# Encoder block on one core: the down projection's right-hand block sums are made in the up projection's rounds and kept in DRAM, and VectorE does all two-operand work of the down projection

## The chip, the core and the metric

The kernel runs on one core of a Trainium2 chip. A core has TensorE (PE; its weight loads, PEld, run beside its matmuls), VectorE (DVE), ScalarE (ACT), GpSimd (POOL) and SyncE (SP), which issues all DMAs of this kernel in one queue. The metric is the device time of one execution in microseconds. The kernel before takes 1479.98 us, the median of three runs (1477.62, 1479.98, 1480.10).

## The reference

One encoder layer on 1024 tokens of width 1024, in float32: a mixer (convolution group and grouped attention), cross-attention into 256 memory tokens, and a gated MLP, each between two RMS norms. The change lies in the MLP:

```
u = h @ w_up                           # 1024 x 1024 by 1024 x 5632
u = depthwise_conv3(u) + b             # along the tokens
y = (gelu(u[:, :2816]) * u[:, 2816:]) @ w_down     # 2816 x 1024
x = x + rmsnorm(y, norm_ffn_post)
```

## The kernel before

Every float32 product is done as three matmuls of rounded parts: an operand x is split into hi (a cast on ScalarE) and lo = x - hi (a subtraction of two operands), and hi*hi, hi*lo and lo*hi are summed in PSUM.

Both MLP products use Winograd's form of Strassen's method on one level: seven products of half-size blocks instead of eight, at the price of sums of blocks.

**Up projection** (lines 829 to 845). Round fi of 22 makes 128 gate and 128 value channels for all tokens. `up_first(fi)` loads wg and starts two products (p1, p2); `up_operands(fi)` loads wv, builds four weight sums s12 and s34 on GpSimd (lines 775 to 778) and splits them (`a_split`, lines 741 to 743: the cast on ScalarE, lo on VectorE or GpSimd); a22, the split of wv's second half, lies in one tile for an even and the next odd round. `up_finish(fi - 1)` runs the five other products p6, p5, p3, p7, p4 of the round before, adds them up on VectorE from PSUM (line 803), does the convolution of three taps (lines 792 to 795), the gelu and the gating, and stores the result to act_d in DRAM. A product is 12 matmuls of 128x512.

**Down projection** (lines 850 to 1020). Products m1, m2, m6, m7, m5, m4, m3 follow one another. Each runs over 11 steps i; a step has one operand tile `op` (hi and lo of a left block, 128x512, and of a right block), used by 4 x 3 matmuls. `operands(name, i)` makes it. The left blocks come from `acts[i]`, read back from act_d, and are changed in place between products. The right blocks are b11, b12, b22, b21 of w_down and four sums of them: t1 = b12 - b11, b22 - b12, t2 = b22 - t1 and t2 - b21. b11 of all steps stays in SBUF (`t1s`, three tiles of the pool `act`) and becomes t1 in m6; the other blocks are staged per step (`stage_w`: two blocks) or per two steps (`stage_pair`: one block), and the sums are made there, on GpSimd and VectorE. From the fourth step on, the lo part of the right block is made on GpSimd (`engs`). The `done` functions add each product's PSUM into the Y tiles on VectorE; `y_half` squares a half for the norm and multiplies it by the gain, `y_out` scales, adds the residual and stores.

**Buffers.** `raw` has 3 tiles of 128x1024 (wg, wv, and staged blocks), `tmp` 4 (q, s12, s34, staged blocks, residuals), `w` 7 of 128x2048 (operands; up to four of them are Y tiles, so three are left for `op` from m6 on), `act` 15 of the same size. PSUM has four tiles of one bank (`psB`) and two of two banks. A framework orders each engine's instructions when the program is built, by the order in which the kernel names them and by its own estimate of when each can start; a tile is loaded again when its last reader has released it. On the chip each engine, SP's queue too, runs its instructions in that order and waits on semaphores.

Of the kernel before, what the change touches and what calls it, by code (L numbers as in the profile page):

```python
# [17 lines left out]
NF = 22  # L18
# [15 lines left out]
def encoder_block(ctx: ExitStack, tc: tile.TileContext, x, xT, mem, w_a, w_q, w_kv, w_mkv, w_mqT,  # L34
# [30 lines left out]
    def f(t):  # L65
        return t.bitcast(F32)
# [673 lines left out]

    def a_split(dst, src, eng):
        nc.scalar.copy(out=dst[:, 0, :], in_=src)  # L742
        eng.tensor_tensor(out=dst[:, 1, :], in0=src, in1=f(dst[:, 0, :]), op=ALU.subtract)  # L743
# [95 lines left out]
    for fi in range(NF + 1):  # L839
        if fi < NF:  # L840
            if fi >= UP_PRE:
                up_first(fi)
            up_operands(fi)
        if fi:
            up_finish(fi - 1)

# [5 lines left out]
    t1s, acts = [], []  # L852
    for i in range(NH):
        if i % 4 == 0:
            n = min(4, NH - i)
            t1s.append(A([4, 512], "t1s", F32))
            nc.sync.dma_start(out=t1s[-1][:, :n, :], in_=w_down[i:i + n, :, 0, :].rearrange("i p n -> p i n"))
        acts.append(A([4, 512], "acts", F32))
        nc.sync.dma_start(out=acts[i][:, 0:2, :], in_=act_d[i].rearrange("p (h t) -> p h t", h=2))
# [6 lines left out]
    def t1_of(i):  # L866
        return t1s[i // 4][:, i % 4, :]

    nst = [0]

    pairs = {}

    def stage_pair(i, b):

        if i % 2 == 0:
            n = min(2, NH - i)
            st = raw("st2").rearrange("p (i n) -> p i n", i=2)
            nc.sync.dma_start(out=st[:, :n, :], in_=w_down[i:i + n, :, b, :].rearrange("i p n -> p i n"))
            pairs[b] = st
        return pairs[b][:, i % 2, :]  # L880

    def stage_w(i, b, n):
        nst[0] += 1
        st = (tmp if nst[0] % 2 == 0 else raw)("st").rearrange("p (b n) -> p b n", b=2)
        nc.sync.dma_start(out=st[:, :n, :], in_=w_down[i, :, b:b + n, :])
        return st
# [6 lines left out]
    def operands(name, i):  # L893
        a11, a21, a12, a22 = [acts[i][:, b, :] for b in range(4)]
        t1 = t1_of(i)
        engs = (V_, V_ if i < 3 else P_)
        if name == "m1":
            s_, t_ = a11, t1
        elif name == "m2":
            s_, t_ = a12, stage_pair(i, 3)  # L900
        elif name == "m6":
            st = stage_w(i, 1, 2)
            comb(P_, t1, st[:, 0, :], t1)
            comb(V_, st[:, 1, :], st[:, 1, :], t1)
            s_, t_ = a11, st[:, 1, :]
        elif name == "m7":
            st = stage_w(i, 1, 2)
            comb(P_, st[:, 1, :], st[:, 1, :], st[:, 0, :])
            comb(V_, a11, a22, a11)
            s_, t_ = a11, st[:, 1, :]  # L910
        elif name == "m5":
            comb(P_, a21, a21, a22, ALU.add)
            s_, t_ = a21, t1
        elif name == "m4":
            st = stage_w(i, 2, 2)
            comb(P_, st[:, 0, :], st[:, 0, :], t1)
            comb(V_, st[:, 0, :], st[:, 0, :], st[:, 1, :])
            s_, t_ = a22, st[:, 0, :]
        else:
            s_, t_ = a12, stage_pair(i, 2)  # L920
        op = (A if name == "m3" and i >= NH - 3 else W)([4, 512], "op")
        for n, src in ((0, s_), (2, t_)):
            nc.scalar.copy(out=op[:, n, :], in_=src)  # L923
            comb(engs[n // 2], op[:, n + 1, :], src, f(op[:, n, :]))
        if name == "m2":
            comb(V_, a11, a22, a11)
            comb(P_, a11, a11, a21, ALU.add)
            comb(V_, a12, a12, a11)
# [35 lines left out]
    def y_half(t, n, y, dst=None):  # L964

        nc.scalar.activation(out=gF[:, 1, H0], in_=y, func=AF.Square, accum_out=ssF[n][:, t:t + 1])
        comb(V_ if n else P_, y if dst is None else dst, y, gF[:, 0, n * 512:n * 512 + 512], ALU.mult)
# [119 lines left out]
```

## Time and profile before

| | us |
|---|---|
| the profiled execution's own time | 1478.46 |
| its span, first to last instruction | 1476.7 |
| TensorE, matmuls | 1392.0 busy (94%) |
| VectorE | 1099.4 busy (74%) |
| ScalarE | 700.5 busy (47%) |
| GpSimd | 707.2 busy (48%) |
| mean granted TensorE clock | 0.983 of full speed |

Busy times are shares of the whole span, in which stages with different limits follow one another; the MLP's two products run from about 770 us to the end. Matmuls overlap one another in the records (0.39 us each, while they start closer together), so TensorE's pace is read from start to start. A wait row names who ended the wait. A group of instructions is named by its line and by the tiles that it writes and reads; line 891 is a helper (`comb`) that makes most two-operand work of the down projection, and line 743 is the second half of `a_split`.

### The profile page before, as it was taken

The numbers are of one execution on the slowest core, as the hardware profiler recorded it, in microseconds if no ns is written. First come the engines' busy times: TensorE is split into PE (matmuls) and PEld (weight loads), VectorE is DVE, ScalarE is ACT, GpSimd is POOL, SyncE is SP. The second block draws the span as 40 slices with busy tenths as digits, with TensorE's granted clock in tenths as the row PEclk, the third lists the DMA queues.
The fourth block names the chain that finished last, engine by engine and source line by source line (L and its number), as shares of the span: only waits on it lengthen the run. The fifth ranks groups of instructions, "written<-read, shape, count | busy, mean of one in ns | idle before, by whom it ended". The sixth has DMA issues, their size and how long they took to land.

```text
span 1476.7 us, 18881 instructions
## 1 busy us (share of the span) xinstructions
PE 1392.0 (94%) x7020; PEld 1165.0 (79%) x7020; DVE 1099.4 (74%) x1323; ACT 700.5 (47%) x1192; POOL 707.2 (48%) x627
## 2 busy tenths in 40 slices
PE   7999999889999999999997999999999997978895
PEld 5889988678988888888875888888888875756784
DVE  7499898899999534335468777777777789996676
ACT  6325653688888424334435444444444443323442
POOL 6628787711111414002137555444445449697456
PEclk9999999999999999999998999999999999999998
DMA  6316770000000524013223222222222292334145
GB/s 208 128 48 207 260 237 15 20 1 1 1 2 29 178 94 141 31 43 129 93 79 114 87 86 86 86 87 86 86 87 79 95 375 100 106 130 143 42 130 192
DMA packets 49515, 152.77 MB, mean 103 GB/s; under 512 B 9104, under 2 KB 9360, under 8 KB 49424
## 3 DMA queue, kind: packets, MB, share of 16 engines
q1 hardware_dynamic: 49424, 151.58, 30.8%
q8 instruction: 55, 0.90, 0.3%
q14 instruction: 36, 0.29, 0.1%
HBM read 119.05 MB, written 32.51 MB: 103 GB/s over the span
## 4 chain that ended last, share of the span: by engine, by line
PE 65%; DVE 15%; POOL 6%; issue 5%; DMA 5%; ACT 3%; SPq 0%; POOLq 0%; DVEq 0%; ACTq 0%
PE p L97 9%; PE p L98 9%; PE p L100 9%; DVE op L891 4%; PE y L98 4%; PE y L100 4%; PE y L97 4%; PE pPT L81 3%; PE sc L100 2%; PE sc L97 2%; PE sc L98 2%; DVE acts L891 2%; PE po L555 2%; PE sp L524 2%; PE sp L525 2%
## 5 line engine op out<-in xcount | busy, mean ns | idle before, releaser
L91 PE MATMUL yd<-op 128*128 128x512 f32 x308 | 126.8, 413 | 31.9 <-DVE op L891 16.0
L295 DVE SCALAR_TENSOR_TENSOR cacc<-conv,col,cacc 128x1009 f32<-128x1009 f32 (+14 forms) x120 | 145.8, 1273 | 4.7 <-ACT cacc L242 4.5
L92 PE MATMUL yd<-op 128*128 128x512 f32 x308 | 123.4, 404 | 1.8 <-DVE op L891 1.7
L923 ACT CAST op<-acts 128x512 fp32r<-128x512 f32 x77 | 47.6, 621 | 129.9 <-PE yd L92 47.6
L891 DVE TENSOR_TENSOR op<-acts,op 128x512 fp32r<-128x512 f32 x77 | 88.7, 1158 | 26.0 <-ACT op L923 25.8
L742 ACT CAST a<-s 128x512 fp32r<-128x512 f32 x88 | 50.6, 620 | 113.4 <-PE p L100 55.4
L91 PEld LDWEIGHTS yd<-op 128*128 128x128 f32 x308 | 60.2, 196 | 55.1 <-POOL op L891 23.5
L90 PE MATMUL yd<-op 128*128 128x512 f32 x308 | 98.4, 394 | 0.0
L743 POOL TENSOR_TENSOR a<-wg,a 128x512 fp32r<-128x512 f32 x44 | 62.5, 1441 | 72.9 <-ACT a L742 72.9
L793 DVE SCALAR_TENSOR_TENSOR c<-u,col,c 128x1023 f32<-128x1023 f32 x44 | 56.7, 1288 | 49.4 <-ACT c L792 49.3
L743 DVE TENSOR_TENSOR a<-s,a 128x512 fp32r<-128x512 f32 x88 | 72.3, 835 | 27.8 <-ACT a L742 27.5
L545 DVE TENSOR_TENSOR PL<-pPT,PH 128x512 fp32r<-128x512 f32 x128 | 82.7, 680 | 5.0 <-ACT PH L544 4.6
L85 POOL TENSOR_SCALAR rt<-ss 128x1 f32<-128x1 f32 (+1 forms) x43 | 13.0, 302 | 150.4 <-ACT x L609 75.8
L527 DVE TENSOR_REDUCE nm<-sp 128x1 f32<-128x1024 f32 x64 | 78.0, 1219 | 2.9 <-PE sp L525 1.8
L530 ACT ACTIVATE P<-sp,nm 128x1024 f32<-128x1024 f32 x64 | 72.2, 1128 | 8.9 <-PE pPT L81 5.1
L792 ACT ACTIVATE c<-u,col 128x1024 f32<-128x1024 f32 x44 | 53.2, 1210 | 48.7 <-DVE u L803 46.8
L544 ACT CAST PH<-pPT 128x512 fp32r<-128x512 f32 x128 | 69.3, 593 | 13.5 <-PE pPT L81 12.7
L92 PEld LDWEIGHTS yd<-op 128*128 128x128 f32 x308 | 60.1, 195 | 16.2 <-DVE op L891 4.2
L81 PE MATMUL pPT<-ident,P 128*128 128x128 f32 x512 | 68.6, 274 | 3.7 <-DVE PL L545 2.3
L90 PEld LDWEIGHTS yd<-op 128*128 128x128 f32 x308 | 58.8, 191 | 12.6
L81 PEld LDWEIGHTS pPT<-ident,P 128*128 128x128 f32 x512 | 58.6, 140 | 12.3 <-DVE PL L545 3.9
L743 POOL TENSOR_TENSOR a<-wv,a 128x512 fp32r<-128x512 f32 x22 | 31.9, 1468 | 74.6 <-ACT a L742 60.5
(352 smaller groups left out, 4553.7 us busy)
## 6 DMA issues: line engine op xcount, KB each, us to landing
st<-in_w_down_dram SPq DMA_DIRECT2D x43, 512.0 KB, 3.8
wg<-in_w_up_dram SPq DMA_DIRECT2D x22, 512.0 KB, 4.1
wv<-in_w_up_dram SPq DMA_DIRECT2D x22, 512.0 KB, 3.9
act_d<-u SPq DMA_DIRECT2D x22, 512.0 KB, 2.9
acts<-act_d SPq DMA_DIRECT2D x22, 512.0 KB, 9.1
wmkv_r<-in_w_mkv_dram SPq DMA_DIRECT2D x16, 512.0 KB, 4.0
x_d<-x SPq DMA_DIRECT2D x16, 512.0 KB, 2.9
wmq_r<-in_w_mqT_dram SPq DMA_DIRECT2D x8, 512.0 KB, 3.5
```

Of the source, the lines that this page charges most:

```text
L81: nc.tensor.transpose(out=out_, in_=in_, identity=ident)
L90: nc.tensor.matmul(out=ps, lhsT=sh, rhs=mh, start=first, stop=False)
L91: nc.tensor.matmul(out=ps, lhsT=sh, rhs=ml, start=False, stop=False)
L92: nc.tensor.matmul(out=ps, lhsT=sl, rhs=mh, start=False, stop=last)
L97: nc.tensor.matmul(out=p, lhsT=sh, rhs=mh, start=first, stop=False)
L98: nc.tensor.matmul(out=p, lhsT=sh, rhs=ml, start=False, stop=False)
L100: ins = nc.tensor.matmul(out=p, lhsT=sl, rhs=mh, start=False, stop=last)
L295: nc.vector.scalar_tensor_tensor(out=acc[:, t0:t1_], in0=a[:, t0 + o:t1_ + o], scalar=cc(C_DW + c * 31 + j), in1=acc[:, t0:t1_], op0=ALU.m ...
L527: nc.vector.reduce_max(out=nm, in_=sp, axis=AX.X, negate=True)
L545: nc.vector.tensor_tensor(out=PL[dst], in0=p3, in1=f(PH[dst]), op=ALU.subtract)
L743: eng.tensor_tensor(out=dst[:, 1, :], in0=src, in1=f(dst[:, 0, :]), op=ALU.subtract)
L891: eng.tensor_tensor(out=dst, in0=in0, in1=in1, op=op)
```

## The change

In each up round a load brings a 256-column half of the four blocks of w_down for one step (`wd`, a tile of `raw`), four subtractions on VectorE turn them in place into the four sums, and a store puts them into a new DRAM array T_d. In program order the load stands after `up_operands(fi)`, the sums and the store after `up_finish(fi - 1)`. In the down projection each product reads the one right block that it needs, from w_down or from T_d, one load for two steps, into `tmp` and `raw` tiles in turn; `t1s`, `stage_w` and the sums of right blocks are gone. The left combinations are made in m2 (three) and m7 (one); m5 has none any more. All splits, the combinations and the gains run on VectorE.

```diff
@@ -738,6 +738,22 @@
 
     act_d = drp.tile([NF, 128, 1024], F32, name="act_d")
 
+
+    T_d = drp.tile([NF // 2, 128, 4, 512], F32, name="T_d")
+
+    wds = {}
+
+    def down_load(fi):
+        wds[fi] = raw("wd").rearrange("p (b n) -> p b n", b=4)
+        nc.sync.dma_start(out=wds[fi], in_=w_down[fi // 2, :, :, fi % 2 * 256:fi % 2 * 256 + 256])
+
+    def down_sums(fi):
+        wd = wds.pop(fi)
+        b11, b12, b22, b21 = [wd[:, b, :] for b in range(4)]
+        for dst, in0, in1 in ((b11, b12, b11), (b12, b22, b12), (b22, b22, b11), (b21, b22, b21)):
+            nc.vector.tensor_tensor(out=dst, in0=in0, in1=in1, op=ALU.subtract)
+        nc.sync.dma_start(out=T_d[fi // 2, :, :, fi % 2 * 256:fi % 2 * 256 + 256], in_=wd)
+
     def a_split(dst, src, eng):
         nc.scalar.copy(out=dst[:, 0, :], in_=src)
         eng.tensor_tensor(out=dst[:, 1, :], in0=src, in1=f(dst[:, 0, :]), op=ALU.subtract)
@@ -841,20 +857,19 @@
             if fi >= UP_PRE:
                 up_first(fi)
             up_operands(fi)
+            down_load(fi)
         if fi:
             up_finish(fi - 1)
+        if fi < NF:
+            down_sums(fi)
 
 
 
 
     NH = NF // 2
     TAIL = 4
-    t1s, acts = [], []
+    acts = []
     for i in range(NH):
-        if i % 4 == 0:
-            n = min(4, NH - i)
-            t1s.append(A([4, 512], "t1s", F32))
-            nc.sync.dma_start(out=t1s[-1][:, :n, :], in_=w_down[i:i + n, :, 0, :].rearrange("i p n -> p i n"))
         acts.append(A([4, 512], "acts", F32))
         nc.sync.dma_start(out=acts[i][:, 0:2, :], in_=act_d[i].rearrange("p (h t) -> p h t", h=2))
     for i in range(NH):
@@ -863,27 +878,20 @@
     nc.sync.dma_start(out=gF[:, 0, :], in_=rows[R_FFNPOST:R_FFNPOST + 1, :].to_broadcast([128, 1024]))
     ssF = (ss1, rstd1)
 
-    def t1_of(i):
-        return t1s[i // 4][:, i % 4, :]
-
-    nst = [0]
-
-    pairs = {}
-
-    def stage_pair(i, b):
+    RHS = {"m1": (w_down, 0), "m2": (w_down, 3), "m6": (T_d, 2), "m7": (T_d, 1), "m5": (T_d, 0), "m4": (T_d, 3),
+           "m3": (w_down, 2)}
+    nst, pair = [0], [None]
+
+    def right(name, i):
 
         if i % 2 == 0:
             n = min(2, NH - i)
-            st = raw("st2").rearrange("p (i n) -> p i n", i=2)
-            nc.sync.dma_start(out=st[:, :n, :], in_=w_down[i:i + n, :, b, :].rearrange("i p n -> p i n"))
-            pairs[b] = st
-        return pairs[b][:, i % 2, :]
-
-    def stage_w(i, b, n):
-        nst[0] += 1
-        st = (tmp if nst[0] % 2 == 0 else raw)("st").rearrange("p (b n) -> p b n", b=2)
-        nc.sync.dma_start(out=st[:, :n, :], in_=w_down[i, :, b:b + n, :])
-        return st
+            src, b = RHS[name]
+            nst[0] += 1
+            st = (tmp if nst[0] % 2 == 0 else raw)("st").rearrange("p (i n) -> p i n", i=2)
+            nc.sync.dma_start(out=st[:, :n, :], in_=src[i:i + n, :, b, :].rearrange("i p n -> p i n"))
+            pair[0] = st
+        return pair[0][:, i % 2, :]
 
     V_, P_ = nc.vector, nc.gpsimd
 
@@ -892,39 +900,17 @@
 
     def operands(name, i):
         a11, a21, a12, a22 = [acts[i][:, b, :] for b in range(4)]
-        t1 = t1_of(i)
-        engs = (V_, V_ if i < 3 else P_)
-        if name == "m1":
-            s_, t_ = a11, t1
-        elif name == "m2":
-            s_, t_ = a12, stage_pair(i, 3)
-        elif name == "m6":
-            st = stage_w(i, 1, 2)
-            comb(P_, t1, st[:, 0, :], t1)
-            comb(V_, st[:, 1, :], st[:, 1, :], t1)
-            s_, t_ = a11, st[:, 1, :]
-        elif name == "m7":
-            st = stage_w(i, 1, 2)
-            comb(P_, st[:, 1, :], st[:, 1, :], st[:, 0, :])
+        t_ = right(name, i)
+        if name == "m7":
             comb(V_, a11, a22, a11)
-            s_, t_ = a11, st[:, 1, :]
-        elif name == "m5":
-            comb(P_, a21, a21, a22, ALU.add)
-            s_, t_ = a21, t1
-        elif name == "m4":
-            st = stage_w(i, 2, 2)
-            comb(P_, st[:, 0, :], st[:, 0, :], t1)
-            comb(V_, st[:, 0, :], st[:, 0, :], st[:, 1, :])
-            s_, t_ = a22, st[:, 0, :]
-        else:
-            s_, t_ = a12, stage_pair(i, 2)
+        s_ = {"m1": a11, "m2": a12, "m6": a11, "m7": a11, "m5": a21, "m4": a22, "m3": a12}[name]
         op = (A if name == "m3" and i >= NH - 3 else W)([4, 512], "op")
         for n, src in ((0, s_), (2, t_)):
             nc.scalar.copy(out=op[:, n, :], in_=src)
-            comb(engs[n // 2], op[:, n + 1, :], src, f(op[:, n, :]))
+            comb(V_, op[:, n + 1, :], src, f(op[:, n, :]))
         if name == "m2":
-            comb(V_, a11, a22, a11)
-            comb(P_, a11, a11, a21, ALU.add)
+            comb(V_, a21, a21, a22, ALU.add)
+            comb(V_, a11, a21, a11)
             comb(V_, a12, a12, a11)
         return op
 
@@ -964,7 +950,7 @@
     def y_half(t, n, y, dst=None):
 
         nc.scalar.activation(out=gF[:, 1, H0], in_=y, func=AF.Square, accum_out=ssF[n][:, t:t + 1])
-        comb(V_ if n else P_, y if dst is None else dst, y, gF[:, 0, n * 512:n * 512 + 512], ALU.mult)
+        comb(V_, y if dst is None else dst, y, gF[:, 0, n * 512:n * 512 + 512], ALU.mult)
 
     def y_out(t, ys):
         rs = sm(1, "rs")
```

## Rows read from the trace of the kernel before

**Rows 1.** Stretches: us, busy PE, PEld, DVE, ACT, POOL (count), clock, DMA share, GB/s.
```profile
801.00:1205.30 404.30, 404.20 (x1783) 334.00 (x1782) 295.90 (x349) 171.49 (x235) 198.68 (x151) 1.00 0.32 106
1205.30:1465.60 260.30, 226.60 (x925) 176.42 (x923) 215.31 (x204) 98.31 (x186) 187.89 (x128) 0.97 0.39 132
840.00:1188.00 348.00, 347.95 (x1535) 287.84 (x1535) 249.20 (x292) 144.79 (x199) 167.30 (x126) 1.00 0.27 89
```

**Rows 2.** Order of time on TensorE, an up round: start us, us, operation.
```profile
1036.64 0.39 PE L97 MATMUL p<-t4h,a 128*128 128x512 f32 x1
...
1039.36 0.39 PE L97 MATMUL p<-b11h,a 128*128 128x512 f32 x1
```

**Rows 3.** TensorE's waits from 1195 us on: total us, times, longest.
```profile
PE yd L91 <- DVE op L891: 16.0, 8, 3.5
PE yd L91 <- POOL op L891: 15.5, 12, 5.1
```

**Rows 4.** Order of time on VectorE, in m1 and at m2's end.
```profile
1228.03 1.77 DVE L891 TENSOR_TENSOR op<-acts,op 128x512 fp32r<-128x512 f32 x1
1229.72 1.77 DVE L891 TENSOR_TENSOR acts<-acts 128x512 f32<-128x512 f32 x1
...
1281.38 0.68 DVE L891 TENSOR_TENSOR op<-st,op 128x512 fp32r<-128x512 f32 x1
1281.98 0.68 DVE L891 TENSOR_TENSOR st<-st,t1s 128x512 f32<-128x512 f32 x1
```

**Rows 5.** Order of time on GpSimd, in the same stretches.
```profile
1225.81 1.74 POOL L891 TENSOR_TENSOR op<-t1s,op 128x512 fp32r<-128x512 f32 x1
...
1285.68 1.75 POOL L891 TENSOR_TENSOR t1s<-st,t1s 128x512 f32<-128x512 f32 x1 [5.99 <-DMA st<-in_w_down_dram]
```

**Rows 6.** The chain that ended last, in m7: start us, us, what.
```profile
1342.00 4.68 DMA st<-in_w_down_dram
```

**Rows 7.** VectorE by line, up rounds 840 to 1188: busy us, mean ns | idle before.
```profile
L743 DVE TENSOR_TENSOR a<-s,a 128x512 fp32r<-128x512 f32 x74 | 61.4, 840 | 22.6 <-ACT a L742 22.6
L793 DVE SCALAR_TENSOR_TENSOR c<-u,col,c 128x1023 f32<-128x1023 f32 x36 | 46.4, 1289 | 46.0 <-ACT c L792 46.0
```

**Rows 8.** VectorE by line, attention: two operands, 256 columns.
```profile
L571 DVE TENSOR_TENSOR o<-o,pRb 128x256 f32<-128x256 f32 x16 | 6.7, 416 | 0.4
```

**Rows 9.** SyncE's loads in order of time, two up rounds.
```profile
1014.88 0.33 SPq L617 DMA_DIRECT2D wg<-in_w_up_dram  x1
1023.59 0.33 SPq L617 DMA_DIRECT2D wv<-in_w_up_dram  x1
...
1027.14 0.37 SPq L617 DMA_DIRECT2D wg<-in_w_up_dram  x1
...
1047.35 0.37 SPq L617 DMA_DIRECT2D wv<-in_w_up_dram  x1
1053.63 0.33 SPq L617 DMA_DIRECT2D wg<-in_w_up_dram  x1
```

**Rows 10.** GpSimd in order of time, the last readers of those loads.
```profile
1022.26 1.30 POOL L777 TENSOR_TENSOR s<-wg,wv 128x512 f32<-128x512 f32 x1
...
1024.89 1.29 POOL L778 TENSOR_TENSOR s<-wg,s 128x512 f32<-128x512 f32 x1
...
1043.06 1.29 POOL L778 TENSOR_TENSOR s<-wg,s 128x512 f32<-128x512 f32 x1
1052.31 1.29 POOL L743 TENSOR_TENSOR a<-wv,a 128x512 fp32r<-128x512 f32 x1 [7.97 <-ACT a L742]
```

**Rows 11.** ScalarE in order of time, the first readers of two wg.
```profile
1031.40 1.14 ACT L742 CAST a<-wg 128x512 fp32r<-128x512 f32 x2 [0.53 <-PE p L100]
...
1055.94 1.13 ACT L742 CAST a<-wg 128x512 fp32r<-128x512 f32 x2
```

**Rows 12.** DMA issues, 840 to 1188: xcount, KB each, median us to landing.
```profile
act_d<-u SPq DMA_DIRECT2D x18, 512.0 KB, 2.9
wv<-in_w_up_dram SPq DMA_DIRECT2D x17, 512.0 KB, 4.1
```

## The prediction

> **What bounds the kernel now.** I read the stretches first, then who TensorE waits for, then the engines' order of time in the two stretches that the change touches.
>
> The up projection (801 to 1205.3 us) keeps TensorE busy for 404.20 of 404.30 us [rows 1]: it sets the pace there. Its pitch is read off two matmul starts: twelve matmuls, one product of 128x512, take 1039.36 - 1036.64 = 2.72 us, 0.2267 us each [rows 2]. A round has 7 products, so 84 matmuls and 19.04 us.
>
> The down projection has 7 x 11 x 4 x 3 = 924 matmuls. At the same pitch they need 209.5 us; the stretch (1205.3 to 1465.6) took 260.3 us at a mean clock of 0.97 [rows 1]. **So 50.8 us of the down projection are not matmul pitch**, and they are all that a change of operand making can win there. TensorE's waits in it name both makers of operands, VectorE with 16.0 us and GpSimd with 15.5 us [rows 3]; what the waits don't name is mostly the weight load that waits first, and the lower clock after a long stall.
>
> Why are the two makers late? A VectorE subtraction of two SBUF operands takes 1.77 us and is followed after 1.69 us while GpSimd works (the first two of [rows 4]), and GpSimd's own takes 1.74 then (the first of [rows 5]). Where GpSimd has no instruction (it waits 5.99 us for a load), the same subtraction lasts 0.68 and starts every 0.60 us (the last of [rows 4, 5]). So one operation handed to GpSimd costs VectorE about 1.1 us, nearly the two operations it could have done itself. Third, the chain that ended last passes through waits for staged blocks of the right-hand weights, four of 3.6 to 4.7 us between 1328 and 1353 (the longest in [rows 6]), each followed by GpSimd's block sum and GpSimd's split.
>
> **The change, part by part.**
>
> *Down projection, VectorE.* After the change GpSimd keeps only the small reciprocal roots and two 128x512 additions there. VectorE has 154 splits, 33 combinations in m2, 11 in m7, 28 sums of PSUM into Y, 16 gains: 242 operations at 0.605 us, 146 us; with 14 of line 981 and 8 small ones some 158 us, of 209.5. It no longer bounds a product on the average: a step has 2 x 0.605 = 1.21 us for TensorE's 2.72, m7 1.8. Only m2, with five per step, needs 3.03 and so 11 x 0.31 = 3.4 us too much; part of it can be done in m1, whose VectorE is more than half empty.
>
> *Down projection, loads.* m6, m7 and m4 load two blocks per step before (33 loads); now every product loads one block per two steps, 42 loads in all, alternating over 3 + 4 buffers of which each serves two steps, and nothing stands between the load and the split. The waits of [rows 6] go. I cost the loads at nothing: seven buffers are 14 steps, 38 us of matmuls.
>
> *What is late next.* After a product the sums into Y come together: 4 x 0.605 = 2.4 us, in m5 eight, 4.8 us, while from m6 on three operand buffers give TensorE about two steps, 5.4 us, less the 1.9 us from a free buffer to two splits (an ACT cast of 0.62, then the subtraction, the second pair overlapping). I leave 4 us for six borders, 3 for the start of m1 (VectorE still ends the last two rounds' convolutions there), 2 for m2, 3 for m3, where line 981 and the roots run in between: 12 us in all (ends: 4, and 30 if the operand chain stays late by half as much as now). Gain 50.8 - 12 = 38.8 us. The last 11.1 us after the last matmul start [rows 1] I leave as they are; line 981 beside GpSimd's two additions stays (ends: 1.5 less, 1 more).
>
> *Up projection, VectorE.* Each of 22 rounds gets four dependent subtractions of 128x256. No row has exactly this; a 128x256 two-operand one with a PSUM input took 0.416 [rows 8]. Alone I take 0.34 apart (its 0.416 less the 0.075 by which 0.68 exceeds 0.605), 1.4 us a round. Beside GpSimd, scaled as 512 columns are (1.69 for 0.605), 0.95 each, 3.8 us a round. VectorE is busy 249.2 of 348.0 us in the middle rounds [rows 1], so it idles 5.4 us of a round, 2.5 of it in the wait for the first convolution step alone (46.0 us before 36 of them [rows 7]). Even 3.8 us fit. What can cost is where the block stands: the evacuations of PSUM behind it in VectorE's order free the four banks for the next products. Ends: 0, and 3.8 x 21 = 80 us with no cover at all. The nearest row is the idle time, so I take 0.3 us a round, 6 us, and 1.5 us for the first round, where VectorE is nearly full.
>
> The Trainium skill, page "GPSIMD Engine Reference", section "Key points", says that GpSimd shares its SBUF interfaces with VectorE and contends with VectorE instructions of two SBUF inputs. That speaks for the down projection and against the sums, which are of that kind and now stand beside GpSimd's up-projection work; the trace has it in the splits of the up rounds, 0.840 us on the mean [rows 7] against 0.68 alone [rows 4]. By that rule alone every sum would be the slow one, 3.8 us a round; by the row, which mixes, about a quarter more than alone, 1.7.
>
> *Up projection, buffers and queue.* The raw ring has three buffers, and wd now passes through it beside wg and wv. Over a pair of rounds (38.1 us, so 114 us of buffer time) I follow each load to its last reader. Rounds 14 and 15: wg issued at 1014.88 is released by line 778 at 1044.35; wv of 1023.59 by the split of line 743 at 1053.60; wg of 1027.14 by line 778 a period after 1026.2, at 1064.3; wv of 1047.35 by line 777 a period after 1023.56, at 1061.7 [rows 9, 10]. That is 29.5 + 30.0 + 37.2 + 14.3 = 111 of 114 us: full, and three of the five loads shown follow a release by at most 1 us. But much of it is waiting after landing (a load takes 4.1 us [rows 12]): wg of 1014.88 lands by 1019.0 and is first read at 1031.40, wg of 1027.14 by 1031.2 and is read at 1055.94 [rows 9, 11]. Without these 37 us, 74 are needed. wd needs 4.1 to land, 1.4 to 3.8 for the sums and 2.9 for its store to land [rows 12], say 11, twice 22: 96 of 114. It fits, if prefetch is given up. (wd and its store move 1 KB runs where wg moves 4 KB and act_d the same; no row shows such runs, and at twice both landings it would be 110, just full.) SP's queue is in order, and a store that waits for its sums holds the loads behind it; the longest such hold before, within the 20 us between two loads from 1027.14 to 1047.35 [rows 9], costs TensorE nothing. Taken: nothing beyond the 0.3 us a round above.
>
> The Trainium skill, page "DMA: Bandwidth & Descriptors", section "Anatomy of one DMA", warns that completion can be surprisingly long when the write goes to HBM. This trace differs: the stores of act_d land in 2.9 us, the loads in 4.1 [rows 12]. By the rule the ring would be held longer; at twice a store's 2.9 it would be 102 of 114 us, which fits too.
>
> *Sum.* 1476.7 - 38.8 + 6 + 1.5 = 1445.4 us of span; the profiled execution's own time is 1.8 us over its span, so 1447.2. That execution (1478.46) is 1.5 us under the median of the runs shown, inside their spread of 2.5, and I don't correct for it: **1447 us**.
>
> **The rivals.** *The ring starves TensorE: slower.* If wd takes its buffer ahead of the next wg, as the program's order has it, it can come in only when the wv of an even round is released, at 1053.60 in the pair above; the next wg then waits for the store, 11 us, and its splits end 4 + 3.2 us later, near 1072 instead of 1058. TensorE starts that product at 1058.4 (1039.36 [rows 2] and a round of 19.04); it may take five older products first, which gives 13.6 us, and that is the lateness itself: no margin. From 1.8 us of stall a round the whole gain is gone (38.8 - 1.5 = 37.3 over 21 rounds); at 2.5 us, 52 in place of the 6, the time is 1494. For: the full ring. Against: the 37 us of idle holding that can be given back. *The up rounds eat most of it:* 0.8 to 1.8 us a round from VectorE's order and the odd late wd, 17 to 37 us in place of 6, time 1458 to 1478, middle 1468. *The down projection wins less:* another link (ACT's casts in order, three operand buffers, the bursts of sums) keeps TensorE waiting; residual 28 instead of 12, 1463. That the change doesn't do what it says gets no chance: the operations that leave GpSimd are counted from the code.
>
> **How the numbers follow.** Forecast 0.58 (its own range 1434 to 1458), smaller gain 0.14, eaten 0.12, ring 0.16. A measurement of this kernel can tell about 0.2%, 3 us, from no change. Of the eaten case 0.09 is faster, 0.02 the same and 0.01 slower. Faster: 0.58 + 0.14 + 0.09 = 0.81; same 0.02; slower 0.16 + 0.01 = 0.17. The low end: residual 5, nothing in the up rounds, the tail 1 less, 1432, rounded to 1434; the high end goes into the ring case, to 1484.
>
> **What would show it.** Right: TensorE still busy over 99% in the up stretch and its rounds 19.0 us; the down stretch, first to last of its 924 matmuls, near 222 us; subtractions there at 0.68 us without a slow kind; no wait for a staged load of w_down or T_d in the chain; GpSimd under 25 us busy in it. Wrong: up rounds of 20 us or more with TensorE waiting for an a1 split or a PSUM bank; or subtractions still at 1.7 us; or the down stretch above 240 us.

## The result, and the profile after

The changed kernel takes 1469.47 us, the median of four runs (1467.17 to 1470.58), beside 1479.41 us for the kernel before on the same chip: a ratio of 0.9932, interval 0.9916 to 0.9947. It is 10 us faster where I forecast 32. The two stretches that the change touches moved by 42 and 50 us in opposite directions, and what is left is their difference. From the start of the first matmul to the start of the last of each:

| us | before | after | forecast |
|---|---|---|---|
| up projection (1848 matmuls) | 435.7 | 478.0 | 443.2 |
| down projection (924 matmuls) | 260.3 | 210.3 | 221.5 |
| from the last matmul's start to the end | 11.1 | 11.4 | 11.1 |

The same two stretches as in [rows 1], in the same columns (us, busy PE, PEld, DVE, ACT, POOL with counts, clock, DMA share, GB/s), for the kernel after:

```profile
801.00:1205.30 404.30, 379.25 (x1620) 307.69 (x1619) 303.83 (x393) 154.71 (x216) 182.29 (x137) 0.98 0.41 134
1205.30:1465.60 260.30, 248.67 (x1087) 204.45 (x1085) 196.17 (x308) 115.60 (x210) 24.34 (x26) 0.99 0.46 161
```

In the first row TensorE, busy for 404.20 us before, now stands for 25 us, and 163 fewer matmuls fall into the window; they come at the start of the second. GpSimd has fallen from 187.89 to 24.34 us in the second row. That row still holds the last up rounds; the down projection by itself, in the same columns:

```profile
1246.70:1457.10 210.40, 209.92 (x925) 173.10 (x924) 156.21 (x254) 98.12 (x184) 10.48 (x13) 1.00 0.41 140
```

VectorE, which makes nearly everything there now, is busy for 156.21 us of it; the forecast was some 158.

VectorE by line, down projection after (busy us, mean ns, idle before):

```profile
L899 DVE TENSOR_TENSOR op<-acts,op 128x512 fp32r<-128x512 f32 x75 | 51.5, 687 | 45.5 <-ACT op L909 45.4
L899 DVE TENSOR_TENSOR op<-st,op 128x512 fp32r<-128x512 f32 x75 | 51.2, 683 | 2.8 <-ACT op L909 2.8
```

The 1.77 us subtractions of [rows 4] are gone: the mean is 0.68 to 0.69, the length that they had where GpSimd was still. Against 924 x 0.2267 = 209.5 us the stretch loses 0.8 us.

Now the up rounds. Who TensorE, VectorE and SP's queue wait for, 801 to 1246 us (us in total, times, longest):

```profile
PE p L97 <- DVE q L819: 19.7, 9, 3.0
PE p L97 <- ACT a L758: 4.4, 2, 2.9
PE p L97 <- DVE u L819: 3.6, 2, 3.1
DVE wd L754 <- DMA wd<-in_w_down_dram: 40.8, 15, 5.0
SPq L748 <- POOL a L759: 47.1, 9, 5.3
```

The last row is SP's queue, holding a load of wd. How the waits come about is seen in order of time (start us, us): VectorE first, then GpSimd beside it, SP's queue, and TensorE's one stall of that stretch:

```profile
1000.50 1.29 DVE L809 SCALAR_TENSOR_TENSOR c<-u,col,c 128x1023 f32<-128x1023 f32 x1 [1.28 <-ACT c L808]
1003.57 1.54 DVE L754 TENSOR_TENSOR wd<-wd 128x256 f32<-128x256 f32 x1 [1.78 <-DMA wd<-in_w_down_dram]
1005.03 0.68 DVE L819 TENSOR_TENSOR q<-p,q 128x512 f32<-128x512 f32 x1
```
```profile
1003.57 1.25 POOL L791 TENSOR_TENSOR s<-wv 128x512 f32<-128x512 f32 x1
```
```profile
999.80 0.57 SPq L748 DMA_DIRECT2D wd<-in_w_down_dram  x1
1010.22 0.55 SPq L755 DMA_DIRECT2D T_d<-wd  x1
```
```profile
1005.85 0.47 PE L97 MATMUL p<-b21h,a 128*128 128x512 f32 x1 [3.00 <-DVE q L819]
```

The load of wd is issued at 999.80, when GpSimd's split, the last reader of a tile of `raw`, has released its buffer (the last row of the waits). It takes 3.8 us to land. VectorE reaches the first subtraction at 1001.8, waits 1.78 us for the landing, and then the subtraction itself lasts 1.54 us where its length alone is 0.41 (below): GpSimd runs a weight sum of line 791 from 1003.57 to 1004.82. The subtraction ends 0.29 us after it. Behind it in VectorE's order stands the sum of line 819 that empties a PSUM bank, and TensorE waits for that bank. In the up rounds there are twelve holes of 0.9 to 3.5 us between matmul starts, 30 us over the pitch. Ten of them end on a sum of line 819, the first two (3.3 and 1.9 us, at 813 and 835 us) on a split that ScalarE made late. Six of them are followed by a stretch of 3.4 us in which the granted clock is 1.2 in place of 2.4 GHz, which costs 1.7 us each, 10 us. That makes 40 of the 42.3. One such stretch, in the columns of the stretches above, with TensorE busy throughout and the clock at 0.50:

```profile
1049.10:1052.50 3.40, 3.40 (x10) 2.62 (x9) 3.37 (x5) 2.49 (x3) 2.23 (x2) 0.50 0.00 0
```

ScalarE has a late split for another reason too. From 890 us on, in every second round, the store of act_d goes out right behind three loads and lands in 6.3 to 8.2 us (2.9 in most rounds before); until then it holds the buffer that the next a1 takes, and ScalarE's split of wg waits for it. In the hole that ends at 900.13 this would have left TensorE some 2 us even without VectorE: the matmul before started at 896.65 and the split was ready at 898.95. In the nine other holes behind a VectorE sum, the sum came 0.4 us or more after the splits.

All subtractions of line 754 in the up rounds (duration in ns: min/median/max):

```profile
L754 DVE TENSOR_TENSOR wd<-wd x86: 406/424/1539, 800.7 to 1215.8; 128x256 f32<-128x256 f32 x86
```

Of these, 34 have no GpSimd instruction beside them and take 406 to 426 ns; the 52 with one for more than a third of their time have a median of 914 and reach 1539. The mean is 721, between the 0.34 and 0.95 us that the prediction took as ends.

### The profile page after: what moved, and what is told of

Its sections match the earlier page's. It is cut to its first block, busy times and chain, and to the rows that moved or that the text cites. A ratio compares the mean times of both kernels' runs of the same rounds, so it can differ in the third digit from the quotient of the medians.

```text
span 1468.5 us, 18850 instructions
## 1 busy us (share of the span) xinstructions
PE 1391.3 (95%) x7020; PEld 1168.7 (80%) x7020; DVE 1083.4 (74%) x1464; ACT 699.1 (48%) x1192; POOL 522.3 (36%) x508
## 4 chain that ended last, share of the span: by engine, by line
PE 48%; DVE 20%; DMA 12%; issue 8%; POOL 7%; ACT 4%; SPq 1%; DVEq 0%; POOLq 0%; ACTq 0%
DMA wd<-in_w_down_dram 5%; PE yd L91 4%; PE yd L92 4%; PE yd L90 4%; PE y L98 4%; PE y L100 4%; PE y L97 4%; DVE wd L754 3%; PE pPT L81 3%; DMA T_d<-wd 2%; PE sc L100 2%; PE sc L97 2%; PE sc L98 2%; DVE u L819 2%; PE sp L524 2%
## 5 line engine op out<-in xcount | busy, mean ns | idle before, releaser
L91 PE MATMUL yd<-op 128*128 128x512 f32 x308 | 119.9, 390 | 0.5 <-DVE op L899 0.5
L92 PE MATMUL yd<-op 128*128 128x512 f32 x308 | 119.7, 389 | 0.0
L754 DVE TENSOR_TENSOR wd<-wd 128x256 f32<-128x256 f32 x88 | 63.8, 725 | 55.0 <-DMA wd<-in_w_down_dram 40.8
L90 PE MATMUL yd<-op 128*128 128x512 f32 x308 | 97.1, 389 | 0.0
L899 DVE TENSOR_TENSOR op<-acts,op 128x512 fp32r<-128x512 f32 x77 | 52.9, 687 | 45.5 <-ACT op L909 45.4
L759 DVE TENSOR_TENSOR a<-s,a 128x512 fp32r<-128x512 f32 x88 | 59.4, 694 | 12.3 <-ACT a L758 12.3
L91 PEld LDWEIGHTS yd<-op 128*128 128x128 f32 x308 | 57.8, 188 | 13.2 <-DVE op L899 1.3
L90 PEld LDWEIGHTS yd<-op 128*128 128x128 f32 x308 | 57.8, 188 | 12.0
L92 PEld LDWEIGHTS yd<-op 128*128 128x128 f32 x308 | 57.8, 188 | 12.0
```

What stands on the lines that cost most here:

```text
L90: nc.tensor.matmul(out=ps, lhsT=sh, rhs=mh, start=first, stop=False)
L91: nc.tensor.matmul(out=ps, lhsT=sh, rhs=ml, start=False, stop=False)
L92: nc.tensor.matmul(out=ps, lhsT=sl, rhs=mh, start=False, stop=last)
L754: nc.vector.tensor_tensor(out=dst, in0=in0, in1=in1, op=ALU.subtract)
```

## Experiments

Each ran in four executions (the split back on GpSimd in ten) in turn with the kernel before; ratios are to that, with the 95% interval. "Up" and "down" are the stretches of the table above.

### The halves apart

**Down projection alone**: no load of wd, no sums, no store; the four blocks of T_d are read from w_down (block b in place of the sum).

```diff
-            down_load(fi)
-        if fi < NF:
-            down_sums(fi)
-    RHS = {... "m6": (T_d, 2), "m7": (T_d, 1), "m5": (T_d, 0), "m4": (T_d, 3), ...}
+    RHS = {... "m6": (w_down, 2), "m7": (w_down, 1), "m5": (w_down, 0), "m4": (w_down, 3), ...}
```

> The down projection's half of the change alone: no wd load, no sums, no store; the products that read T_d read blocks of w_down instead (so the values differ, the work does not). All theories: up stretch back to 404 us, down stretch 211 us for its 924 matmuls as in the changed kernel, time 1428 (1469.5 less the 41 us by which the up rounds grew). If the down stretch needed the late, stretched last rounds of the up projection to get ahead with its operands, it would lose 5 to 15 us again: 1433 to 1443.

Measured: 1427.53 us, 0.9643 (0.9628 to 0.9658); up 436.1, down 209.5: as expected, and nothing over the matmul pitch in the down projection.

**Up projection alone**: the kernel before with load, sums and store of wd added to its rounds, and the old down projection.

```diff
             up_operands(fi)
+            down_load(fi)
         if fi:
             up_finish(fi - 1)
+        if fi < NF:
+            down_sums(fi)
```

> The up rounds' half alone: wd load, four sums, store to T_d; the down projection as before, T_d unread. If the two halves add up: up stretch 441 to 446 us as in the changed kernel, time 1479 + 41 = 1520. If the old down projection hides part of it (its operands get ahead while TensorE waits in the up rounds): 1505 to 1515.

Measured: 1524.02 us, 1.03 (1.0274 to 1.0326); up 474.8, down 266.9. The halves add up: -53 and +44 us against the kernel before give -9 for the measured -10.

### Ring, queue or VectorE

**No subtractions**: wd is loaded and stored, the four subtractions are left out.

```diff
-        for dst, in0, in1 in ((b11, b12, b11), (b12, b22, b12), (b22, b22, b11), (b21, b22, b21)):
-            nc.vector.tensor_tensor(out=dst, in0=in0, in1=in1, op=ALU.subtract)
```

> The changed kernel without the four subtractions of a round; wd is loaded and stored as it is (left out: the sums, so T_d holds plain blocks). Theory A (VectorE's queue: the sums wait there for wd and hold back the sums out of PSUM, which TensorE waits for): the up rounds lose at most 8 us, time 1430 to 1436. Theory B (the raw ring: with wd in it wg comes too late for the a1 split): up rounds still lose over 25 us, time 1455 to 1468. Theory C (VectorE has too much to do beside GpSimd): as A, 1430 to 1436.

**Own buffers**: wd in the two halves of a tile of its own in place of `raw`.

```diff
-        wds[fi] = raw("wd").rearrange("p (b n) -> p b n", b=4)
+        wds[fi] = own[:, fi % 2 * 2:fi % 2 * 2 + 2, :].rearrange("p a (c n) -> p (a c) n", c=2)
```

> The changed kernel with wd in two buffers of its own (one tile of the act pool, halves in turn), so the raw ring holds wg and wv alone as before. Theory A with the late load as its root, and theory B: the wait for wd goes, up rounds lose at most 8 us, time 1430 to 1437. Theory A with the sums badly placed however early wd comes, and theory C: still 20 us or more lost, 1450 to 1468.

Measured: without subtractions 1433.51 us, 0.9682 (0.9664 to 0.9701), up 442.5. So the third load in the ring, the store in SP's queue and their bandwidth cost 6.8 us, and **36 us hang on the subtractions**. With buffers of their own 1463.71 us, 0.9883 (0.986 to 0.9905), up 474.3, in the second of the two ranges: the wait for wd fell from 40.8 to 15.7 us, but the framework now put all 88 subtractions between 803 and 967 us, with holes of up to 6.4 us from 815 to 982 us and none later. So loads that pass through a full ring don't starve TensorE; whether wd's lateness at VectorE costs it, this run doesn't tell.

**Time without waiting** and **waiting without time**: the subtractions work on a resident tile of ones, or on 4 of 256 columns.

```diff
-        b11, b12, b22, b21 = [wd[:, b, :] for b in range(4)]
+        b11, b12, b22, b21 = [own[:, b, fi % 2 * 256:fi % 2 * 256 + 256] for b in range(4)]   # first
+        b11, b12, b22, b21 = [wd[:, b, 0:4] for b in range(4)]                                 # second
```

> The load of wd and the store of T_d stay; the four subtractions of a block keep their size and their number, but read and write a resident tile of ones, so that they never wait for wd (the blocks in DRAM are then raw w_down, and the output is not the reference's). Theory A1 (the subtractions cost by their wait for wd, with what is queued behind them on VectorE): the up projection ends near 1212 to 1217 us and the time is 1433 to 1441 us. Theory A2 (VectorE's own time, 4 x 0.72 us a block, put ahead of the PSUM sums and splits in its order): the up projection still ends at 1232 us or later and the time is 1453 us or more.

> The subtractions are made on 4 of the 256 columns only, so they wait for wd as before but take VectorE hardly any time (the other columns of the blocks are raw w_down, and the output is not the reference's). A1 (the wait for wd): the up projection still ends at 1235 us or later and the time is 1456 us or more. A2 (VectorE's own time): it ends near 1213 to 1220 us and the time is 1436 to 1443 us. Between the two, each has its share.

Measured: 1435.78 us, 0.9713 (0.9697 to 0.9729), up 441.4; and 1485.19 us, 1.004 (1.0025 to 1.0055), up 494.5. The first missed its question: having no load to wait for, all 88 subtractions were placed ahead of the up rounds, at 664 to 725 us. The second lies in A1's range but not for A1's reason: with 64 times fewer columns and only 5.1 us of waiting for wd in all, the rounds lost 59 us. VectorE by line in its up rounds:

```profile
L754 DVE TENSOR_TENSOR wd<-wd 128x4 f32<-128x4 f32 x84 | 63.9, 760 | 8.9 <-DMA wd<-in_w_down_dram 5.1 <-POOL a L759 2.5
```

Four columns take 760 ns on the mean, as long as 256 did. The 24 without a GpSimd instruction beside them take about 152, the 60 beside one 1186 (medians). So the price is set by what GpSimd is doing, and a third theory (A3) was needed: VectorE stands still until GpSimd's instruction is over, and all that is queued behind stands with it. The trace shows it: in eight rounds the four of a block now stand one after the other, ahead of a sum of line 819, for example here (start us, us).

```profile
896.88 3.90 DVE L754 TENSOR_TENSOR wd<-wd 128x4 f32<-128x4 f32 x4
900.69 0.68 DVE L819 TENSOR_TENSOR u<-p,q 128x512 f32<-128x512 f32 x1
```

TensorE's hole of 3.4 us ends at 901.5, behind that sum. TensorE's waits for the sums of line 819 into u are 23.9 us in all, where the changed kernel has 3.6.

**One operand**: a block is multiplied by 1.0 (two strided halves) instead of subtracted.

```diff
-            nc.vector.tensor_tensor(out=dst, in0=in0, in1=in1, op=ALU.subtract)
+            nc.vector.tensor_scalar(out=dst.rearrange("p (n two) -> p two n", two=2), in0=in0.rearrange(...),
+                                    scalar1=1.0, scalar2=None, op0=ALU.mult)
```

> The four instructions of a block stay on VectorE at their places, wait for the same load and run over the same 256 columns (in two strided halves), but read one SBUF operand in place of two: a block is multiplied by 1.0, so that T_d holds raw w_down and the output is not the reference's. Theory A3 (a VectorE instruction with two SBUF operands stands still while a GpSimd instruction runs, up to 1.5 us, and what is queued behind it on VectorE is late): these instructions take about 0.42 us beside GpSimd too, the up projection ends at 1213 to 1225 us and the time is 1436 to 1448 us, the rest over the kernel without subtractions being the wait for wd. Theories A1 and A2 (the wait for wd, VectorE's own time): the loss stays, the up projection ends at 1238 us or later and the time is 1460 us or more.

Measured: 1490.29 us, 1.0063 (1.0047 to 1.0079), up 494.8. The expectation failed in its premise: alone the instruction took 0.28 us against the subtraction's 0.41, and beside GpSimd it stood as before, median 1.23 us. Less the 0.15 us that 4 columns take, 0.28 is half of the subtraction's time for a column (an estimate from these three figures). So this instruction, at about double the rate, is held up although it reads one operand, and the time, though in the range of A1 and A2, says nothing against A3.

**Reduction**: sums over pairs of columns of one operand, 256 columns read, in the place of the subtraction. The instructions of all engines keep the order of the changed kernel, so this is the run that separates standing still from order.

```diff
-            nc.vector.tensor_tensor(out=dst, in0=in0, in1=in1, op=ALU.subtract)
+            nc.vector.tensor_reduce(out=dst[:, :128], in_=in0.rearrange("p (n two) -> p n two", two=2), op=ALU.add, axis=AX.X)
```

> Each subtraction is replaced by a sum over pairs of columns of one operand (256 columns read, 128 written; the output is not the reference's). The order of all engines is that of the changed kernel, and the instructions wait for the same load. A3 (VectorE stands still beside GpSimd because of the second SBUF operand): the reductions take 0.3 to 0.45 us beside GpSimd as well, the up projection ends at 1213 to 1228 us (the rest over 1210.7 being the wait for wd), the time is 1436 to 1452 us. If the place in VectorE's order and the wait for wd decide: the up projection still ends at 1240 us or later and the time is 1464 us or more.

Measured: 1452.59 us, 0.9811 (0.979 to 0.9832), up 459.8. Its instructions in the up rounds and the line by line view:

```profile
L754 DVE TENSOR_REDUCE wd<-wd x85: 404/414/422, 801.0 to 1199.7; 128x128 f32<-128x256 f32 x85
```
```profile
L754 DVE TENSOR_REDUCE wd<-wd 128x128 f32<-128x256 f32 x85 | 35.3, 415 | 51.1 <-DMA wd<-in_w_down_dram 43.1 <-POOL a L759 3.8 <-DMA act_d<-u 3.7
```

Never longer than 422 ns, 54 of them beside a GpSimd instruction. With the same order and the same wait for wd (43.1 us), the up projection is 18.2 us shorter: that is what standing still cost. The end, 1228.8, and the time, 1452.59, lie just past the 1228 and 1452 that A3 allowed, since the wait for wd was dearer than I had put it. Of the eleven holes that TensorE still has in these rounds, nine end within 4 us of a reduction for which VectorE had stood idle, 1.8 to 4.7 us each.

**Reduction without the wait**: the same, reading the round's wv, which has landed long before, and writing to a tile of its own; wd is loaded and stored as before.

```diff
-        b11, b12, b22, b21 = [wd[:, b, :] for b in range(4)]
+        b11, b12, b22, b21 = [rvs[fi][:, b * 256:b * 256 + 256] for b in range(4)]
-            nc.vector.tensor_reduce(out=dst[:, :128], ...
+            nc.vector.tensor_reduce(out=own[:, fi % 4, :128], ...
```

> As the run with reductions, but they read the round's wv, which is there long before, and write to a tile of their own; wd is still loaded and stored (the output is not the reference's). So VectorE has the same 88 instructions of 0.42 us without the wait for wd and without the standing still. If the wait for wd is what is left of the loss: the up projection ends at 1211 to 1217 us and the time is 1433 to 1440 us. If VectorE's own 36 us are: it ends at 1223 us or later and the time is 1446 us or more.

Measured: 1432.82 us, 0.9676 (0.966 to 0.9692), up 438.7. VectorE by line, its up rounds:

```profile
L761 DVE TENSOR_TENSOR a<-s,a 128x512 fp32r<-128x512 f32 x85 | 73.7, 888 | 20.6 <-ACT a L760 20.6
L756 DVE TENSOR_REDUCE own<-wv 128x128 f32<-128x256 f32 x88 | 36.5, 415 | 1.7
```

VectorE does the same 36.5 us of additional work, its splits (first line) are slowed by GpSimd as much as ever, and the rounds lose 3.0 us; time and end (1209.6) lie just under the first range. The order of its instructions is not that of the run before it, so the 21.1 us between the two are the wait together with what the framework does when it need not plan for one. Against the run without subtractions the reductions cost 459.8 - 442.5 = 17.3 us.

### GpSimd in the down projection

**The split back on GpSimd**: the changed kernel with the low part of the right operand on GpSimd from the fourth step on.

```diff
-            comb(V_, op[:, n + 1, :], src, f(op[:, n, :]))
+            comb(P_ if n and i >= 3 else V_, op[:, n + 1, :], src, f(op[:, n, :]))
```

> The changed kernel with one thing of the old down projection put back: GpSimd makes the low part of the right operand for i >= 3 (133 instructions of some 1.25 us), VectorE the rest. VectorE gets 90 us less work there. If GpSimd's instructions beside VectorE were what the down projection lost, its loss of 1 us comes back in good part, 15 to 45 us, and the time is 1484 to 1515 us. If the loss came from the chained sums of blocks, it stays under 5 us and the time is 1467 to 1474 us.

**All on VectorE, nothing moved**: the kernel before, with one word changed.

```diff
-    V_, P_ = nc.vector, nc.gpsimd
+    V_, P_ = nc.vector, nc.vector
```

> The kernel before with one word changed: in the down projection every subtraction and addition is made by VectorE, none by GpSimd; the right-hand block sums stay in the down projection, chained as they were, and nothing is added to the up projection. If sharing the work with GpSimd was what the down projection lost: its 924 matmuls take 210 to 222 us, the up projection stays at 436 us, and the time is 1428 to 1441 us, below the changed kernel. If the chain of load, block sum and split was: they still take 240 us or more and the time is 1458 us or more.

Measured: 1476.41 us, 0.9973 (0.996 to 0.9987), down 215.5, a loss of 6.0 that falls between the two expectations; and **1437.37 us, 0.9711 (0.9693 to 0.9728)**, up 436.7, down 218.0. The one word takes 42.3 us off the down projection and adds 1.0 to the up projection. Its stretches and its subtractions:

```profile
801.00:1205.30 404.30, 403.68 (x1778) 333.76 (x1778) 296.80 (x352) 169.91 (x233) 191.16 (x144) 1.00 0.32 105
1205.30:1427.00 221.70, 214.59 (x935) 174.20 (x933) 196.04 (x327) 99.76 (x187) 10.55 (x12) 1.00 0.46 158
```
```profile
L891 DVE TENSOR_TENSOR op<-acts,op 128x512 fp32r<-128x512 f32 x75 | 51.9, 695 | 14.5 <-ACT op L923 14.5
L891 DVE TENSOR_TENSOR st<-st 128x512 f32<-128x512 f32 x22 | 15.4, 698 | 1.0 <-DMA st<-in_w_down_dram 0.9
L891 DVE TENSOR_TENSOR st<-st,t1s 128x512 f32<-128x512 f32 x22 | 15.2, 697 | 3.1 <-DMA st<-in_w_down_dram 3.0
```

The block sums are still there (the last two lines and t1), each at 0.70 us and not at the 1.2 to 1.6 that VectorE's took before; VectorE is busy 196.04 of 221.70 us, though it does the work of both, where it was busy 215.31 of 260.30 with part of it [rows 1]. It is the fastest version here that computes the whole layer, though its interval overlaps that of the nearest one below (token steps, GpSimd). What it still loses, 8.5 us, is all that was to be had by moving the block sums out of the down projection.

### Other places for the sums

**GpSimd in the up rounds**, in place of VectorE (`nc.gpsimd.tensor_tensor` in `down_sums`):

> The four subtractions of a block are made by GpSimd in place of VectorE, in the same rounds. If VectorE is the cause, by A1 or A2, the loss in the up rounds falls from 41 us to under 15 us and the time is 1432 to 1442 us. If the cause is the later store of T_d, which then waits for a slower engine and holds the weight loads queued behind it, or if GpSimd's subtractions slow VectorE beside them, it stays above 1460 us.

**GpSimd in the attention loop**, one block every second step from step 10 on, the up rounds as before (`down_load(n); down_sums(n)` in the loop):

> Load, subtractions (on GpSimd) and store are made in the attention loop instead, one block every second step, and the up rounds are those of the kernel before. If the attention loop has room on GpSimd and on SP's queue: the up projection is as long as before (436 us), the down projection loses nothing, and the time is 1427 to 1433 us. If the loop's own work waits for GpSimd, the loop grows by up to 1.5 us a block, 33 us, and the time is up to 1461 us.

**In the 24 token steps between attention and the up projection**, one block a step, on GpSimd, and the same on VectorE:

> Load, subtractions and store of a block are made on GpSimd in the 24 token steps of the output projection, the memory scores and the memory values (TensorE over 99% busy there, GpSimd 20%, VectorE 40%), one block a step; the up rounds are those of the kernel before. With room there: up projection 436 us, down projection without loss, 1427 to 1434 us. If the ring or the weight loads of these steps are held up: up to 20 us more, as in the attention loop.

> The same steps, but the subtractions on VectorE. By the lock theory they take 0.42 to 1.5 us there too, but VectorE has 60% of its time free and TensorE waits for little from it: 1427 to 1438 us. If VectorE's place in the chain of these steps (norm, split, transposition) decides, 10 to 30 us more.

**Only in the steps that seemed free**, 20 blocks in the scores; 4, 16 and 2 around them; 14 at the end of attention and 8 in the scores:

> Load, subtractions on GpSimd and store of 20 blocks in the eight steps of the memory scores (580 to 680 us, where the run with one block a step lost nothing to 8 blocks), 2 in the last steps of the output projection. With room for 2.5 blocks a step on GpSimd (7 us of 11.7 us) and on the DMA (250 GB/s): 1428 to 1433 us. If the loads of the next weights are late behind them in SP's queue: 5 to 15 us more.

> 4 blocks in the last four steps of the output projection, 16 in the scores (two a step), 2 in the first two steps of the memory values. 1428 to 1434 us; up to 8 us more if the steps ahead of and behind the scores wait for GpSimd as with one block a step.

> Load, subtractions on GpSimd and store of 14 blocks in the last part of the attention loop, where GpSimd is 10% busy and no DMA runs, and of 8 in the scores' steps. If GpSimd's work disturbs nothing there: 1428 to 1434 us. If VectorE (94% busy there) stands still beside it: up to 0.9 us a block, as in the loop's earlier part, 1440 to 1446 us.

| where | us | ratio (interval) | up | down | first up matmul |
|---|---|---|---|---|---|
| up rounds, GpSimd | 1446.81 | 0.9778 (0.9763 to 0.9792) | 451.7 | 213.4 | 767.6 |
| attention, GpSimd | 1447.31 | 0.9782 (0.9768 to 0.9797) | 435.9 | 209.5 | 788.3 |
| token steps, GpSimd | 1441.35 | 0.9735 (0.9718 to 0.9751) | 435.9 | 209.5 | 780.4 |
| token steps, VectorE | 1444.31 | 0.9747 (0.972 to 0.9775) | 436.2 | 209.5 | 787.0 |
| scores | 1455.27 | 0.9835 (0.9816 to 0.9854) | 435.4 | 209.5 | 793.6 |
| around the scores | 1443.04 | 0.9756 (0.9738 to 0.9773) | 436.5 | 209.5 | 783.7 |
| late attention | 1447.95 | 0.9784 (0.9769 to 0.9798) | 435.8 | 209.5 | 789.8 |

The first row went the way expected for a VectorE cause, but above its range: 16.0 us lost in the rounds for "under 15", and 1446.81 us for 1432 to 1442. In the others the rounds are clean, and what they save there the earlier stage pays: its first up matmul, at 769.4 before, comes 11 to 24 us later. None reaches the range that it was given for the case of room, 1438 us at the highest, and none beats the one-word change: a block costs 0.5 us or more wherever I put it. In the scores the next stage's weight loads came late behind stores of T_d in SP's queue; ScalarE waited 27.8 us for the first of them, VectorE 26.0 us for ScalarE's split that stood behind it, and TensorE, which waited for VectorE, had one hole of 18.6 us at 674 us; why the attention's end, with a still DMA and an almost idle GpSimd, paid 20 us I did not follow up.

## Why the prediction was wrong

**Wrong: the up rounds, 6 + 1.5 us forecast, 42.3 measured.** Two steps failed.

*"The nearest row is the idle time, so I take 0.3 us a round, 6 us"*: this step failed first. VectorE's idle time did hold the work: 36.5 us of reductions cost 3.0 us with nothing to wait for. But I priced an instruction by its length and looked for room for it, while what counts is how long it can stand at the head of an in-order engine. Beside GpSimd a subtraction of 0.41 us stands up to 1.5 us; that cost 18.2 us. I had the 0.95 us as an end and called even 3.8 us a round covered.

*"It fits, if prefetch is given up."* and *"Taken: nothing beyond the 0.3 us a round above."* The ring did fit, and gave up its prefetch: SP's queue holds the loads of wd until a buffer is free (47.1 us), each wd is loaded just before it is used, and VectorE waits for the landing, 40.8 us in all. That piece is 17 to 21 us, about as large as the standing still. The loads themselves took 3.6 to 7.9 us to land, where the prediction had 4.1: the long ones went out right behind a wg and a wv. The stores of T_d took 3.2 us on the median for its 2.9. The prediction followed the buffers to their last readers and never asked who would be waiting at the landing, and what was queued behind.

The pieces, each the difference of two runs: 3.0 for load, store and the instructions' own time (6.8 in the run without subtractions, so 3 to 7), 21.1 for the wait (17.3 by that other run, so 17 to 21), 18.2 for standing still, 42.3 together. Only the last is a difference with every engine's order kept; how the rest is shared between the wait and the order that the framework chose is not shown.

**Right in kind, too small: the down projection, 38.8 us forecast, 50.0 measured.** The term that was mis-sized is the 12 us that I kept for borders, m2, the first product and m3: they are 0.8. The reason given held: with GpSimd out, the subtractions last 0.68 to 0.69 us. The runs add which part of the change did it: 42.3 us come from taking GpSimd out of the down projection, which needs no moved sum, and 7.7 from the rest, the block sums that left it and the loads staged another way. GpSimd's split alone brought back 5.2 us, with GpSimd busy 95.8 of 215.8 us. The kernel before had it busy 187.89 of 260.30 [rows 1], and block sums that each engine waited for from the other; how the 42.3 us divide between VectorE's slowed instructions, GpSimd's own slow ones and those hand-overs, no run shows. This gain, larger than forecast, hid 11 us of the first miss.

**Rivals.** "The up rounds eat most of it" had the right place (VectorE's order, the late wd) and nearly the right price, 0.8 to 1.8 us a round for a measured 1.9; with the larger gain below, the time came out inside its 1458 to 1478. It got 0.12. "The ring starves TensorE" had the ring full, as it is (47.1 us of held loads of wd), and a wrong consequence: the splits of wg and wv come late for TensorE in the first two holes (4.4 us of waits) and, by some 2 us, at 900; in the others a sum of VectorE comes last, which is late by wd (without the subtractions the same ring costs 6.8 us). Of the signs given, the 0.68 us subtractions, GpSimd under 25 us (10.48) and the clean down stretch were seen, TensorE's 99% in the up stretch was not (379.25 of 404.30 us); a pair of rounds takes 41.8 us (1002.47 to 1044.23) and TensorE waits for a PSUM bank, the sign against.

The Trainium skill, page "SBUF — State Buffer", section "SBUF: two separate sides", says that the port pair of VectorE and GpSimd is an exclusive lock, held for the whole instruction, not a shared bandwidth, and that it takes VectorE instructions with two SBUF inputs or in a two-port mode. The runs agree: 4 columns stand as long as 256 (medians of 1186 and 914 ns beside GpSimd), one operand at the double rate stands (1.23 us), a reduction does not (422 ns at most). The prediction named the contention and had both prices, "about a quarter more than alone" from the mean of a mixed row and 0.95 us scaled from a slowed one; it held either against the idle time, and not against what stands behind in VectorE's order.

## What to carry to other kernels

Work moved to an idle engine is priced by what stands behind it in that engine's order: by its wait for its own data and by how long it can be held up, not by whether its length fits the idle time. Before a computation is moved out of a stage, take the disturbing engine out of the stage and look again: here one word gave 42 of the 50 us and cost 1. VectorE instructions with two SBUF operands and GpSimd instructions belonged in different stretches here; an operation handed to GpSimd cost VectorE more than it saved (1.77 us in place of 0.68 for the one beside it).

## What was not expected of the hardware

A VectorE instruction on 4 columns took 0.15 us alone and 1.19 beside GpSimd, so a shorter instruction does not lower this price; both runs with shorter instructions lost more than the subtractions themselves (494.5 and 494.8 us of up projection against 478.0), in an order of VectorE's instructions that had also changed; in the run with 4 columns the trace shows the new order at work, four in a row ahead of a PSUM sum. A multiplication by a constant in float32 from SBUF to SBUF, strided by two, took 0.28 us for 256 columns where the subtraction took 0.41, and was held up beside GpSimd (median 1.23 us); a reduction over the same columns took 0.41 us and was not (422 ns at most).
